# Twenty convolution taps behind the attention, and the layer norm's sums behind later output blocks

## The chip, the cores and the metric

The kernel runs on one core of one Trainium2 chip. The metric is the device time of one execution in microseconds (us), as a median over runs. The engines are called PE (matrix multiplication), DVE (vector), ACT (scalar activation), POOL (GpSimd) and SP (which issues DMA loads).

## The reference

Two layers work on 512 tokens of width 1024. Each layer is a half-step SwiGLU network, a mixer, a second half-step SwiGLU network and a norm. The mixer, which is what the change touches, runs three groups of heads side by side and projects them together:

```python
n = rms_norm(h, mix_norm[l])
p = n @ w_in[l]
u_conv, q, k, v, q_mem = jnp.split(p, splits, axis=-1)
y_conv = conv_module(u_conv, ...)   # GLU, causal depthwise conv of 31 taps over 384 channels, layer norm, silu
y_swa = sliding_window_attention(q, k, v, swa_sinks[l])   # 6 query heads, 2 kv heads, window 128
y_mem = memory_attention(qm, mk, mv)                      # 4 heads over 256 memory tokens
y = jnp.concatenate([y_conv, y_swa, y_mem], axis=-1)
h = h + y @ w_out[l]                                      # 1024 x 1024
```

All is in float32.

## The kernel before

**Layout.** Channels lie on the 128 partitions and the 512 tokens along a row. Matrix products in full precision are made of three products of split operands: `mm3` multiplies hi by hi, lo by hi and hi by lo. A weight is split by ACT (`hi`, a rounded copy) and then by DVE (`lo`, the rest), in `split`; with `split_by_dma` ACT makes both copies and an accumulating DMA from POOL adds the weight to the second.

**The mixer.** `ORDER` lists its steps; the last three are `a` (attention), `t` (taps), `s` (swish). The convolution's 384 channels are three tiles `cv[:, 0..2]` of 128 channels. `tap(c, j)` adds tap j to tile c: one DVE instruction over 512 tokens (L947; the first tap of a tile is L944). There are 3 x 31 = 93 taps. `taps` lists them so that mostly two tiles alternate; the first 13 belong to tile 0 alone and the last 18 to tile 2 alone.

The attention goes over ten groups of head pairs (`GROUPS`). For each group PE makes the scores (L785, L779 adds the mask), DVE takes the row maxima (L789, L804), ACT the exponentials (L816), PE transposes (L826), ACT copies back (L828), PE multiplies by the values (L837) into a bank `po`, DVE scales (L849 to L851), PE transposes the result (L860) and ACT and DVE split it (L146, L147) into the operand `y`.

**What sets the order.** Instructions are placed on each engine's queue by a planner, in the order of the program where several are ready. `tc.issue_after(x)` puts an instruction behind x on x's engine, without waiting for it; `queued()` does so behind PE's last product. So PE's order in this stage is that of the program. Taps from number `EARLY` on are put behind `biased[g]`, the DVE instruction that ends the maxima of group g; `LATER` says how many belong to each group.

**The output projection.** It has eight blocks of 128 output channels, d = 0 to 7. The columns of the weight that meet the convolution (`ours`) come last. The other five 128-row pieces of a block are the window heads (`OWN`, three pieces) and the memory heads (`MEMORY`, two); `out_rows(d, rows)` multiplies them into bank `oo[d]`. `out_weights(d)` loads and splits the weight of block d; the split pieces have four buffers, so that of block d + 4 waits until block d is done.

**The layer norm.** `swish` sums the three tiles on POOL (L969, L970), PE multiplies the sum by ones (L974), DVE subtracts the mean (L977), ACT squares, PE sums the squares over channels (L203), POOL takes the power (L194), PE spreads the result to all partitions (L216), ACT copies it (L222), DVE multiplies (L991), ACT applies silu (L992), ACT and DVE split. Output blocks stand between these products in PE's order. Banks: three of `mm`, two of `po`, one `cf`, a ring of two `pt`.

Of the kernel before, what the change touches and what calls it, by code (L numbers as in the profile page):

```python
# [46 lines left out]
ORDER = "c00 c01 c10 c11 q0 q1 q2 q3 Q0 c20 Q1 c21 Q2 v0 v1 Q3 g0 V1 v2 v3 a t s"  # L47

ALONE = 13
EARLY = 62  # L50
LATER = (1, 4, 3, 3, 2, 2, 2, 2, 2)


def cut(v, bits):
# [11 lines left out]
def trunk(ctx: ExitStack, tc: tile.TileContext, xT, memT, pos, w1a, w3a, w2a, w1b, w3b, w2b,  # L66
# [10 lines left out]
    ps_mm = ctx.enter_context(tc.tile_pool(name="ps_mm", bufs=3, space=bass.MemoryType.PSUM))  # L77
    ps_ax = ctx.enter_context(tc.tile_pool(name="ps_ax", bufs=2, space=bass.MemoryType.PSUM))

    turn, tail = [0], [None]  # L80

    def queued():

# [59 lines left out]


    def split(hi, lo, x, on):
        A.activation(hi, x, AF.Copy)  # L146
        on.tensor_tensor(out=lo, in0=x, in1=hi.bitcast(F32), op=ALU.subtract)  # L147

    def split_by_dma(hi, lo, x, src):

# [33 lines left out]
    def blk(k, n=P):  # L184
        return slice(k * n, (k + 1) * n)
# [219 lines left out]
    def ffn(l, w13, w2, x, sums, factors, last, at_product, aside=None, closing=None):  # L405

        def up(f, i):
            ps = bank([P, S], "po" if 2 * f + i in (3, 4) else "mm")  # L410
            project(ps, weights(w13[i][l, f], 1024, V if f == 0 or f < 3 and l == 0 and w13[0] is w1a else G), x)
            return ps

        def gate(pp, R, u, g, hi, lo):
            V.tensor_tensor(out=u, in0=pp[0], in1=R, op=ALU.mult)
            A.activation(u, u, AF.Silu)
            V.tensor_tensor(out=g, in0=pp[1], in1=R, op=ALU.mult)
            V.tensor_tensor(out=g, in0=g, in1=u, op=ALU.mult)
# [12 lines left out]
        while len(products) < at_product:  # L431
            products.append(up(len(products) // 2, len(products) % 2))
        with queued():
            r = sums()
        with queued():
            products.append(up(at_product // 2, at_product % 2))
        with queued():
            gain, R, after = factors(r)
        M = Seven(normed(gain, R))
        with queued():  # L440
            for f in range(0, PLAIN, 2):
                u, v = (tmp.tile([P, 2, S], F32, tag=t, name=t, bufs=n) for t, n in (("u", 1), ("g", 2)))
                for j in range(2):
                    while len(products) < 2 * (f + j) + 2:
                        products.append(up(len(products) // 2, len(products) % 2))
                    gate(products[2 * (f + j) :], R, u[:, j], v[:, j], *g[f + j])
                if not f:
                    M.first()
        M.rest()
        for q, (f0, nf) in enumerate(QUARTERS):  # L450
            ahead = 2 if q + 1 < len(QUARTERS) else 0
            for f in range(f0, f0 + nf + ahead, 2):
                if f not in g:
                    g[f], g[f + 1] = up_pair(l, w13, f, M)
                    if f == PLAIN:
                        with tc.issue_after(M.gated.ins):
                            rescale = after()
            begun = []

            def begin(d):  # L460

                w = weights(w2[l, d, :, f0 * P : (f0 + nf) * P], nf * P, V)
                ps = bank([P, S], "mm")
                for j in range(nf - 2):
                    mm3(ps, at(w, ALL, blk(j)), g[f0 + j], j == 0, False)
                begun.append((ps, w))

            for d in range(KD if ahead or not closing else KD - 2):
                while len(begun) < (d + 1 if ahead or d else 3):
                    with nullcontext() if ahead or d else queued():  # L470
                        begin(len(begun))
                ps, w = begun[d]
                for j in range(nf - 2, nf):
                    mm3(ps, at(w, ALL, blk(j)), g[f0 + j], False, j == nf - 1)
                if not q and rescale:
                    with tc.issue_after((added if d else M.gated).ins):
                        rescale(d)
                added = V.scalar_tensor_tensor(out=h[:, d, :], in0=ps, scalar=0.5, in1=h[:, d, :], op0=ALU.mult, op1=ALU.add)  # L478
                if not ahead:
                    last(d)  # L480
            if closing and not ahead:
                closing(l, f0, nf, g, [at(p, ALL, slice(0, nf * P)) for p in
                                       (weights(w2[l, d, :, f0 * P : (f0 + nf) * P], nf * P, V) for d in range(KD - 2, KD))])
            if aside and not q:
                aside(added)
# [143 lines left out]
    def mixer(l, x, st, last):  # L629
# [12 lines left out]
        scratch = [wst.tile([P, UNIT], F32, tag="aux", name=f"aux{i}", bufs=3) for i in range(3)]  # L642
        uu = tmp.tile([P, 2, S], F32, tag="u", name="uu", bufs=1)
        query = [tmp.tile([P, 2, S], F32, tag="g", name="query", bufs=2) for _ in range(2)]
        rings = {"pr": [uu[:, 0], uu[:, 1], tm("pr", "pr", 1)], "ptb": [scratch[0][:, blk(i, S)] for i in range(2)],
                 "yn": [scratch[1][:, blk(i, CCH)] for i in range(2)], "cv": [scratch[2][:, blk(i, S)] for i in range(2)]}

        def ring(name):
# [11 lines left out]
            return tuple(z.rearrange("p i s -> p (i s)") for z in gated_pair())  # L660


        biased, raised = {}, {}

        def conv_half(c, i):
            nonlocal R
# [88 lines left out]
            with queued():  # L755
                to_columns(qmT[:, :, blk(t)], memory_query(t), 2)

        yy, y = [], []

# [9 lines left out]
        def scored(kind, pairs):  # L769
# [34 lines left out]
                V.tensor_reduce(out=each(nmw, i), in_=pp[i], axis=AX.X, op=ALU.max)  # L804
            V.scalar_tensor_tensor(out=at_(nmw), in0=at_(nmw), scalar=-1.0, in1=rr, op0=ALU.mult, op1=ALU.mult)
            biased[len(biased)] = V.tensor_tensor(out=at_(nmw), in0=at_(nmw), in1=per(nsinks), op=ALU.min)
            G.tensor_tensor(out=at_(esw), in0=at_(nmw), in1=per(sinks), op=ALU.add)
            return pp, W

        def powers(kind, b, c, scores, W):  # L810
# [28 lines left out]
        def scaled(kind, b, po):  # L839

            n = NH if kind == "w" else NM
            rd = sm(n, f"rd{n}", "a", 4)
            if kind == "w":
                e = esw[:, b]
                A.activation(e, e, AF.Exp)
                V.tensor_tensor(out=rd.rearrange("p (c i) -> p i c", i=2), in0=po[:, :, HD].rearrange("p (c i) -> p i c", i=2), in1=e, op=ALU.add)
                V.reciprocal(rd, rd)
            else:
                V.reciprocal(rd, po[:, :, HD])  # L849
            z = ring("yn")[:, 0 : n * HD]  # L850
            V.tensor_tensor(out=heads(z), in0=po[:, :, 0:HD], in1=rd.unsqueeze(2).to_broadcast([P, n, HD]), op=ALU.mult)  # L851
            return z

        def attended(kind, b, z):
# [7 lines left out]
            while c < n:  # L862
                k = CC + c + (0 if kind == "w" else CC)
                m = 2 - k % 2
                hi, lo = at(yy[k // 2], ALL, slice(k % 2, 2), blk(b))
                split(hi, lo, pt[:, c : c + m, :], V)
                c += m

        GROUPS = (("r", (0, 0), (0, 1)), ("r", (1, 0), (1, 1)), ("w", (0, 0), (0, 1), (0, 2)), ("w", (1, 0), (1, 1)), ("w", (2, 0), (2, 1)),
# [7 lines left out]
        def attention():  # L877
# [45 lines left out]
            for r in done:  # L923
                attended(*r)
            out_rows(2, MEMORY)


        OWN, MEMORY = range(CC), range(CC, 5)
        oo, out_w = [], []
# [20 lines left out]
        def taps():  # L950
# [7 lines left out]
            for n, (c, j) in enumerate(turns):  # L958
                n -= EARLY
                group = sum(n >= sum(LATER[:g]) for g in range(1, len(LATER) + 1))  # L960
                with tc.issue_after(biased[group].ins) if n >= 0 else nullcontext():
                    tap(c, j)


# [1 line left out]

        def swish():
            s1 = ring("cv")
            G.tensor_tensor(out=s1, in0=cv[:, 0, :], in1=cv[:, 1, :], op=ALU.add)  # L969
            G.tensor_tensor(out=s1, in0=s1, in1=cv[:, 2, :], op=ALU.add)  # L970
            out_rows(0, OWN)
            pm = bank([P, S], "pt")
            with queued():
                tail[0] = T.matmul(pm, onesq, s1, start=True, stop=True)  # L974
            st = Stat("st")
            for c in range(CC):
                V.scalar_tensor_tensor(out=cv[:, c, :], in0=pm, scalar=-1.0 / CCH, in1=cv[:, c, :], op0=ALU.mult, op1=ALU.add)  # L977
                st.add(cv[:, c, :], last=c == CC - 1)
            out_rows(1, OWN)
            out_rows(2, OWN)  # L980
            out_rows(3, MEMORY)
            with queued():
                r = rms_cols(st, CCH)
            out_rows(3, OWN)
            with queued():
                RL = kept(spread(r), "RL")
            out_weights(4)
            out_rows(4, (*MEMORY, *OWN))
            for c in range(CC):
                s = ring("cv")  # L990
                V.tensor_tensor(out=s, in0=cv[:, c, :], in1=RL, op=ALU.mult)  # L991
                swished.append(A.activation(s, s, AF.Silu, scale=ln_g[:, c : c + 1], bias=ln_b[:, c : c + 1]))  # L992
                split(y[c][0], y[c][1], s, V)
            for d in range(5, KD):
                out_weights(d)
                out_rows(d, (*MEMORY, *OWN))

        for step in ORDER.split():
            f = {"c": conv_half, "q": queries, "Q": query_columns, "v": values, "V": value_columns, "g": begin, "a": attention,
# [8 lines left out]
        for i, own in enumerate(ours):  # L1008
            raw = wst.tile([P, UNIT], F32, tag="raw", name="raw", bufs=3)
            for j in range(2):  # L1010
                nc.sync.dma_start(raw[:, blk(j, CCH)], wout[l, 2 * i + j, :, 0:CCH])
            with tc.issue_after(swished[1].ins if i > 1 else kept.at.ins) if i else nullcontext():
                A.activation(own[0], raw[:, 0 : 2 * CCH], AF.Copy)
                A.activation(own[1], raw[:, 0 : 2 * CCH], AF.Copy, scale=-1.0)
            for j in range(2):
# [183 lines left out]
```

## The time and the profile before

| | |
|---|---|
| median of 3 runs | 1772.33 us (1772.06 to 1772.84) |
| the profiled execution | 1773.87 us, span 1771.7 us |
| granted clock of PE over the span | 0.998 |
| busy share of PE, DVE, ACT, POOL | 99%, 72%, 51%, 11% |
| layer 0's attention, from 446.6 us to 488.6 us | 42.0 us |
| layer 0's output blocks without the convolution's part | 488.6 us to 520.0 us |

An instruction's row in the profile gives its start, its duration, the engine, the line of the kernel, and the tile written and those read; a count (x) merges equal neighbours. Durations of neighbours on an engine overlap a little, so the step from one start to the next is what an instruction costs there. The busy time of PE is modelled from pipelined products.

### The profile page before, as it was taken

To read this page: it belongs to the slowest core of one execution; us is meant where nothing else is said; L and a number is where in the kernel's file an instruction comes from. 1 tells how busy PE (TensorE), PEld (TensorE's weight loads), DVE (VectorE), ACT (ScalarE), POOL (GpSimd) and SP (SyncE) were. 2 spreads that over 40 slices of the span, in tenths; PEclk is the share of its full clock that TensorE was granted. 3 is DMA by queue.
4 is the path that set the end of the run, shared out by engine and by line. 5 is a ranking of instruction groups with operands and counts; after the bars stand their busy time and mean duration, and the time that the engine had idled before them with its cause. 6 is when DMAs were issued, how large, how long until landed. Compare 5 with 4: busy or idle time off the path is not lost.

```text
span 1771.7 us, 28152 instructions
## 1 busy us (share of the span) xinstructions
PE 1750.1 (99%) x11028; PEld 1579.7 (89%) x11028; DVE 1273.9 (72%) x1895; ACT 900.4 (51%) x1371; POOL 196.9 (11%) x220
## 2 busy tenths in 40 slices
PE   8999999999999999999999999999999999999997
PEld 7989999988788989898889898989887889998987
DVE  6969666589947857575678786666898577666755
ACT  6546444365765535353656453545466755353533
POOL 1001000016121000000010010000251210000000
PEclk9999999999999999999999999999999999999999
DMA  9456645266067547465567465642550866574622
GB/s 281 121 162 177 175 133 148 62 191 135 1 177 175 137 138 175 132 170 137 151 141 182 127 179 143 174 124 84 158 127 2 233 136 170 134 179 125 171 75 84
DMA packets 97205, 253.60 MB, mean 143 GB/s; under 512 B 9904, under 2 KB 16304, under 8 KB 97072
## 3 DMA queue, kind: packets, MB, share of 16 engines
q1 hardware_dynamic: 78064, 190.45, 35.4%
q0 software_dynamic: 19008, 61.35, 19.2%
q8 instruction: 87, 1.43, 0.3%
q14 instruction: 46, 0.38, 0.1%
HBM read 249.67 MB, written 2.10 MB: 142 GB/s over the span
## 4 chain that ended last, share of the span: by engine, by line
PE 87%; DVE 9%; ACT 2%; DMA 1%; issue 1%; SPq 0%; DVEq 0%; ACTq 0%
PE mm L177 13%; PE mm L178 12%; PE mm L179 12%; PE po L177 9%; PE po L179 9%; PE po L178 9%; PE pt L177 6%; PE pt L178 6%; PE pt L179 6%; DVE there L947 5%; PE cf L203 1%; PE po L837 1%; DVE nmw L804 1%; DMA raw<-in_wqk 0%; DMA raw<-in_w2b 0%
## 5 line engine op out<-in xcount | busy, mean ns | idle before, releaser
L146 ACT ACTIVATE whi<-raw 128x1024 fp32r<-128x1024 f32 (+3 forms) x346 | 326.3, 946 | 442.5 <-PE mm L178 227.9
L147 DVE TENSOR_TENSOR wlo<-raw,whi 128x1024 fp32r<-128x1024 f32 (+3 forms) x346 | 374.2, 1082 | 137.0 <-ACT whi L146 136.2
L177 PE MATMUL mm<-ghi,whi 128*128 128x512 f32 (+1 forms) x752 | 292.2, 391 | 0.0
L178 PE MATMUL mm<-glo,whi 128*128 128x512 f32 (+1 forms) x752 | 292.1, 388 | 0.0
L179 PE MATMUL mm<-ghi,wlo 128*128 128x512 f32 (+1 forms) x734 | 284.9, 388 | 0.0
L178 PE MATMUL po<-ml,whi 128*128 128x256 f32 x864 | 244.5, 283 | 0.0
L179 PE MATMUL po<-mh,wlo 128*128 128x256 f32 x864 | 244.5, 283 | 0.0
L177 PE MATMUL po<-mh,whi 128*128 128x256 f32 x864 | 244.4, 283 | 0.0
L179 PE MATMUL pt<-xhi,wlo 128*128 128x256 f32 x864 | 243.9, 283 | 0.0
L178 PE MATMUL pt<-xlo,whi 128*128 128x256 f32 x864 | 243.9, 283 | 0.0
L177 PE MATMUL pt<-xhi,whi 128*128 128x256 f32 x864 | 243.3, 283 | 0.1
L478 DVE SCALAR_TENSOR_TENSOR h<-mm,h 128x512 f32<-128x512 f32 x126 | 86.3, 688 | 129.2 <-PE mm L179 129.1
L177 PEld LDWEIGHTS mm<-ghi,whi 128*128 128x128 f32 x752 | 141.4, 188 | 29.2 <-DVE h L478 1.2
L178 PEld LDWEIGHTS pt<-xlo,whi 128*128 128x128 f32 x864 | 165.7, 192 | 0.8
L177 PEld LDWEIGHTS po<-mh,whi 128*128 128x128 f32 x864 | 165.8, 192 | 0.7
L178 PEld LDWEIGHTS po<-ml,whi 128*128 128x128 f32 x864 | 165.8, 192 | 0.6
L178 PEld LDWEIGHTS mm<-glo,whi 128*128 128x128 f32 x752 | 141.4, 188 | 28.0 <-issue 0.5
L177 PEld LDWEIGHTS pt<-xhi,whi 128*128 128x128 f32 x864 | 165.2, 192 | 1.2 <-DVE g L369 0.3
L179 PEld LDWEIGHTS po<-mh,wlo 128*128 128x128 f32 x864 | 165.8, 192 | 0.0
L179 PEld LDWEIGHTS pt<-xhi,wlo 128*128 128x128 f32 x864 | 165.6, 192 | 0.0
L179 PEld LDWEIGHTS mm<-ghi,wlo 128*128 128x128 f32 x734 | 137.9, 188 | 28.4
L947 DVE SCALAR_TENSOR_TENSOR there<-ypad,par,there 128x512 f32<-128x512 f32 x180 | 136.2, 779 | 1.0
(324 smaller groups left out, 3321.5 us busy)
## 6 DMA issues: line engine op xcount, KB each, us to landing
raw<-in_w2a SPq DMA_DIRECT2D x48, 384.0 KB, 3.5
raw<-in_w2b SPq DMA_DIRECT2D x48, 384.0 KB, 3.5
raw<-in_w1b SPq DMA_DIRECT2D x26, 512.0 KB, 3.7
raw<-in_w3b SPq DMA_DIRECT2D x26, 512.0 KB, 4.0
raw<-in_w1a SPq DMA_DIRECT2D x25, 512.0 KB, 3.7
raw<-in_w3a SPq DMA_DIRECT2D x25, 512.0 KB, 3.8
wsum<-in_w1a SPq DMA_DIRECT2D x18, 512.0 KB, 4.5
wsum<-in_w3a SPq DMA_DIRECT2D x18, 512.0 KB, 4.4
```

The lines of the kernel that those rows point to most:

```text
L146: A.activation(hi, x, AF.Copy)
L147: on.tensor_tensor(out=lo, in0=x, in1=hi.bitcast(F32), op=ALU.subtract)
L177: T.matmul(ps, a[0], b[0], start=first, stop=False, **more)
L178: T.matmul(ps, a[0], b[1], start=False, stop=False, **more)
L179: tail[0] = T.matmul(ps, a[1], b[0], start=False, stop=last, **more)
L203: tail[0] = T.matmul(ss[:, t : t + 1], x[:, blk(t)], onec, start=i == t == 0, stop=i == len(st.sums) - 1, skip_group_check=True)
L478: added = V.scalar_tensor_tensor(out=h[:, d, :], in0=ps, scalar=0.5, in1=h[:, d, :], op0=ALU.mult, op1=ALU.add)
L804: V.tensor_reduce(out=each(nmw, i), in_=pp[i], axis=AX.X, op=ALU.max)
L837: tail[0] = T.matmul(po[:, 2 * c + i, :], ptb[:, i, j, :], v, start=(j == 0), stop=(j == nk - 1))
L947: V.scalar_tensor_tensor(out=cv[:, c, :], in0=ypad[:, c, j : j + S], scalar=conv_w[:, c, j : j + 1], in1=cv[:, c, :], op0=ALU.mult, op1=AL ...
```

## The change

- `EARLY` goes from 62 to 59 and `LATER` from 21 taps in all to 14. The next two taps are put behind the attention's last scaling (`ended[-1]`, L851) and the last 18 behind the last split of its results (`turning[-1][1]`, L147).
- The attention's step now ends with the window heads' pieces of blocks 0 to 2, blocks 3 and 4 whole, and the weights of blocks 4 to 7. They stood in `swish`, between the layer norm's products.
- In `swish`, block 5 stands between the mean's product and the column sums, the memory pieces of block 6 between the sums and the spread, the rest of block 6 and block 7 behind it. The column sums use the ring `pt` and not `cf`. A small silu behind the last square brings ACT's table. POOL's first sum goes behind the last group's `esw`. Tile 2's result uses a third buffer.
- The first two pairs of `ours` are copied by ACT behind the attention's last split, the other two behind `swished[2]`, which is now the last split of the result and not the second silu.
- `hold` puts the first weights' split of the next SwiGLU network behind the last subtraction of the mean on DVE, and the second weights' copies behind `swished[2]` on ACT.

```diff
-EARLY = 62
-LATER = (1, 4, 3, 3, 2, 2, 2, 2, 2)
+EARLY = 59
+LATER = (1, 3, 2, 2, 1, 2, 1, 1, 1)
...
         def up(f, i):
             ps = bank([P, S], "po" if 2 * f + i in (3, 4) else "mm")
-            project(ps, weights(w13[i][l, f], 1024, V if f == 0 or f < 3 and l == 0 and w13[0] is w1a else G), x)
+            with tc.issue_after(hold[f].ins) if f in hold else nullcontext():
+                w = weights(w13[i][l, f], 1024, V if f == 0 or f < 3 and l == 0 and w13[0] is w1a else G)
+            project(ps, w, x)
...
             out_rows(2, MEMORY)
-
+            for d in range(4):
+                out_rows(d, (*MEMORY, *OWN) if d > 2 else OWN)
+                out_weights(d + 4)
+            out_rows(4, (*MEMORY, *OWN))
...
-                with tc.issue_after(biased[group].ins) if n >= 0 else nullcontext():
+                behind = biased[group] if group < len(LATER) else ended[-1] if n < sum(LATER) + 2 else turning[-1][1]
+                with tc.issue_after(behind.ins) if n >= 0 else nullcontext():
                     tap(c, j)
...
             s1 = ring("cv")
-            G.tensor_tensor(out=s1, in0=cv[:, 0, :], in1=cv[:, 1, :], op=ALU.add)
+            with tc.issue_after(sunk[-1].ins):
+                G.tensor_tensor(out=s1, in0=cv[:, 0, :], in1=cv[:, 1, :], op=ALU.add)
             G.tensor_tensor(out=s1, in0=s1, in1=cv[:, 2, :], op=ALU.add)
-            out_rows(0, OWN)
             pm = bank([P, S], "pt")
             with queued():
                 tail[0] = T.matmul(pm, onesq, s1, start=True, stop=True)
             st = Stat("st")
             for c in range(CC):
-                V.scalar_tensor_tensor(out=cv[:, c, :], in0=pm, ...)
+                hold[0] = V.scalar_tensor_tensor(out=cv[:, c, :], in0=pm, ...)
                 st.add(cv[:, c, :], last=c == CC - 1)
-            out_rows(1, OWN)
-            out_rows(2, OWN)
-            out_rows(3, MEMORY)
+            out_rows(5, (*MEMORY, *OWN))
             with queued():
-                r = rms_cols(st, CCH)
-            out_rows(3, OWN)
+                r = rms_cols(st, CCH, "pt")
+            with tc.issue_after(st.at.ins):
+                A.activation(sm(1, "silu"), onec, AF.Silu)
+            out_rows(6, MEMORY)
             with queued():
                 RL = kept(spread(r), "RL")
-            out_weights(4)
-            out_rows(4, (*MEMORY, *OWN))
+            out_rows(6, OWN)
             for c in range(CC):
-                s = ring("cv")
+                s = third if c == 2 else ring("cv")
                 V.tensor_tensor(out=s, in0=cv[:, c, :], in1=RL, op=ALU.mult)
-                swished.append(A.activation(s, s, AF.Silu, scale=ln_g[:, c : c + 1], bias=ln_b[:, c : c + 1]))
-                split(y[c][0], y[c][1], s, V)
-            for d in range(5, KD):
-                out_weights(d)
-                out_rows(d, (*MEMORY, *OWN))
+                A.activation(s, s, AF.Silu, scale=ln_g[:, c : c + 1], bias=ln_b[:, c : c + 1])
+                swished.append(split(y[c][0], y[c][1], s, V)[0])
+            hold[1] = swished[2]
+            out_rows(7, (*MEMORY, *OWN))
...
-            with tc.issue_after(swished[1].ins if i > 1 else kept.at.ins) if i else nullcontext():
+            with tc.issue_after(swished[2].ins if i > 1 else turning[-1][0].ins):
                 A.activation(own[0], raw[:, 0 : 2 * CCH], AF.Copy)
```

More of the change, by code (lines that the diff above doesn't have):

```diff
@@ L78, in trunk @@
     ps_ax = ctx.enter_context(tc.tile_pool(name="ps_ax", bufs=2, space=bass.MemoryType.PSUM))
-    turn, tail = [0], [None]
+    turn, tail, hold = [0], [None], {}
     def queued():
@@ L145, in split @@
     def split(hi, lo, x, on):
-        A.activation(hi, x, AF.Copy)
-        on.tensor_tensor(out=lo, in0=x, in1=hi.bitcast(F32), op=ALU.subtract)
+        a = A.activation(hi, x, AF.Copy)
+        return a, on.tensor_tensor(out=lo, in0=x, in1=hi.bitcast(F32), op=ALU.subtract)
     def split_by_dma(hi, lo, x, src):
@@ L449, in ffn @@
         M.rest()
+        hold.clear()
         for q, (f0, nf) in enumerate(QUARTERS):
@@ L644, in mixer @@
         query = [tmp.tile([P, 2, S], F32, tag="g", name="query", bufs=2) for _ in range(2)]
-        rings = {"pr": [uu[:, 0], uu[:, 1], tm("pr", "pr", 1)], "ptb": [scratch[0][:, blk(i, S)] for i in range(2)],
+        third = tm("pr", "pr", 1)
+        rings = {"pr": [uu[:, 0], uu[:, 1], third], "ptb": [scratch[0][:, blk(i, S)] for i in range(2)],
                  "yn": [scratch[1][:, blk(i, CCH)] for i in range(2)], "cv": [scratch[2][:, blk(i, S)] for i in range(2)]}
@@ L660, in spare @@
             return tuple(z.rearrange("p i s -> p (i s)") for z in gated_pair())
-        biased, raised = {}, {}
+        biased, raised, ended, turning = {}, {}, [], []
         def conv_half(c, i):
@@ L756, in value_columns @@
                 to_columns(qmT[:, :, blk(t)], memory_query(t), 2)
-        yy, y = [], []
+        yy, y, sunk = [], [], []
         nmw, esw = (const.tile([P, NT, 2, CC], F32, tag=t, name=t) for t in ("nmw", "esw"))
@@ L806, in scored @@
             biased[len(biased)] = V.tensor_tensor(out=at_(nmw), in0=at_(nmw), in1=per(nsinks), op=ALU.min)
-            G.tensor_tensor(out=at_(esw), in0=at_(nmw), in1=per(sinks), op=ALU.add)
+            sunk.append(G.tensor_tensor(out=at_(esw), in0=at_(nmw), in1=per(sinks), op=ALU.add))
             return pp, W
@@ L850, in scaled @@
             z = ring("yn")[:, 0 : n * HD]
-            V.tensor_tensor(out=heads(z), in0=po[:, :, 0:HD], in1=rd.unsqueeze(2).to_broadcast([P, n, HD]), op=ALU.mult)
+            ended.append(V.tensor_tensor(out=heads(z), in0=po[:, :, 0:HD], in1=rd.unsqueeze(2).to_broadcast([P, n, HD]), op=ALU.mult))
             return z
@@ L865, in attended @@
                 hi, lo = at(yy[k // 2], ALL, slice(k % 2, 2), blk(b))
-                split(hi, lo, pt[:, c : c + m, :], V)
+                turning.append(split(hi, lo, pt[:, c : c + m, :], V))
                 c += m
@@ L976, in swish @@
             for c in range(CC):
-                V.scalar_tensor_tensor(out=cv[:, c, :], in0=pm, scalar=-1.0 / CCH, in1=cv[:, c, :], op0=ALU.mult, op1=ALU.add)
+                hold[0] = V.scalar_tensor_tensor(out=cv[:, c, :], in0=pm, scalar=-1.0 / CCH, in1=cv[:, c, :], op0=ALU.mult, op1=ALU.add)
                 st.add(cv[:, c, :], last=c == CC - 1)
-            out_rows(1, OWN)
-            out_rows(2, OWN)
-            out_rows(3, MEMORY)
+            out_rows(5, (*MEMORY, *OWN))
             with queued():
-                r = rms_cols(st, CCH)
-            out_rows(3, OWN)
+                r = rms_cols(st, CCH, "pt")
+            with tc.issue_after(st.at.ins):
+                A.activation(sm(1, "silu"), onec, AF.Silu)
+            out_rows(6, MEMORY)
             with queued():
                 RL = kept(spread(r), "RL")
-            out_weights(4)
-            out_rows(4, (*MEMORY, *OWN))
+            out_rows(6, OWN)
             for c in range(CC):
-                s = ring("cv")
+                s = third if c == 2 else ring("cv")
                 V.tensor_tensor(out=s, in0=cv[:, c, :], in1=RL, op=ALU.mult)
-                swished.append(A.activation(s, s, AF.Silu, scale=ln_g[:, c : c + 1], bias=ln_b[:, c : c + 1]))
-                split(y[c][0], y[c][1], s, V)
-            for d in range(5, KD):
-                out_weights(d)
-                out_rows(d, (*MEMORY, *OWN))
+                A.activation(s, s, AF.Silu, scale=ln_g[:, c : c + 1], bias=ln_b[:, c : c + 1])
+                swished.append(split(y[c][0], y[c][1], s, V)[0])
+            hold[1] = swished[2]
+            out_rows(7, (*MEMORY, *OWN))
         for step in ORDER.split():
```

## The prediction

> **What bounds the kernel now.** I read the page first (part 1 for the engines, part 4 for the chain), then tables of time windows around one mixer, then the waits of PE there, and last the instructions of each engine in order of time.
>
> ```profile
> PE 1750.1 (99%) x11028; PEld 1579.7 (89%) x11028; DVE 1273.9 (72%) x1895; ACT 900.4 (51%) x1371; POOL 196.9 (11%) x220
> ```
>
> PE is busy for 1750.1 of 1771.7 us, so an edit that leaves PE's instructions as they are can gain only what PE now waits, and loses whatever new wait it gives PE. The table of windows (columns: window, its length, then busy us and instructions of PE, PEld, DVE, ACT, POOL; granted clock; DMA) shows where the waits lie. The first row is layer 0's attention, the second its output blocks up to the convolution's own part, the third 72 products (x73 with one cut at the edge) of that part; the last two are layer 1's attention and output blocks.
>
> ```profile
> 446.60:488.60 42.00, 39.35 (x321) 33.09 (x319) 38.46 (x88) 30.80 (x74) 7.55 (x9) 1.00 0.01 1
> 488.60:520.00 31.40, 31.40 (x151) 25.86 (x151) 13.97 (x23) 17.57 (x26) 9.37 (x10) 1.00 0.57 140
> 520.00:536.30 16.30, 16.30 (x73) 13.49 (x73) 11.59 (x18) 12.11 (x18) 2.59 (x3) 1.00 1.06 291
> 1321.30:1363.50 42.20, 39.46 (x321) 33.13 (x319) 38.64 (x90) 30.96 (x75) 7.57 (x9) 1.00 0.01 1
> 1363.50:1394.90 31.40, 31.40 (x151) 25.83 (x151) 14.74 (x24) 19.07 (x27) 9.37 (x10) 1.00 0.56 140
> ```
>
> The layers are alike, so I work out one and double it. PE waits 42.00 - 39.35 = 2.65 us in the attention and not at all in the output blocks. The waits of PE in the attention's window:
>
> ```profile
> PE pt L826 <- ACT aux L828: 1.3, 2, 0.7
> PE pt L860 <- ACT aux L828: 0.7, 1, 0.7
> PE pt L826 <- DVE glo L147: 0.3, 1, 0.3
> ```
>
> DVE stands behind the first and third: its taps (L947) sit in front of the maxima that ACT needs. Where the taps are now (busy us of that line alone):
>
> ```profile
> 386.00:442.40 56.40, 42.25 (x56) 1.00 0.72 162
> 442.40:481.70 39.30, 18.43 (x25) 1.00 0.01 1
> 481.70:491.10 9.40, 7.45 (x10) 1.00 0.01 2
> ```
>
> With the three first taps (L944) some 59 lie ahead of the first group's maxima, 24 (25 with one cut) within the groups, 10 after the last group's.
>
> **The change, part by part.** *Taps.* 59 stay ahead, 14 lie within, 20 follow: ten leave the attention. Of the 20, two come behind the last scaling (L851) and 18 behind the last split of the attention (L147). Those 18 are the lone channel's, each adding to the result of the one before. The price of such a tap differs from that of alternating channels; DVE in order of time, with POOL's first sum (L969) as the fourth row:
>
> ```profile
> 386.15 2.33 DVE L947 SCALAR_TENSOR_TENSOR there<-ypad,par,there 128x512 f32<-128x512 f32 x3
> 429.48 4.72 DVE L947 SCALAR_TENSOR_TENSOR there<-ypad,par,there 128x512 f32<-128x512 f32 x7
> 461.73 1.64 DVE L947 SCALAR_TENSOR_TENSOR there<-ypad,par,there 128x512 f32<-128x512 f32 x1
> 461.56 1.26 POOL L969 TENSOR_TENSOR aux<-there 128x512 f32<-128x512 f32 x1
> ```
>
> Three dependent taps take 2.33, so with 0.75 for the last the step is (2.33 - 0.75) / 2 = 0.79; seven alternating ones give (4.72 - 0.74) / 6 = 0.66. I use 0.79.
>
> *The attention.* What it can give is between 0 and 2.65 us a layer. The 0.7 before L860 is the last group's copy out of the bank and has no tap in front, so I take the rest, 2.65 - 0.75 = 1.9.
>
> *PE's cover behind it.* The change puts output blocks 0 to 4 ahead of the mean's product (L974). PE before, in order of time:
>
> ```profile
> 486.60 0.44 PE L860 MATMUL pt<-cst,aux 128*128 128x128 f32 x2 [0.75 <-ACT aux L828]
> 488.58 0.48 PE L177 MATMUL mm<-ghi,whi 128*128 128x512 f32 x1
> 491.46 0.55 PE L860 MATMUL pt<-cst,aux 128*128 128x128 f32 x3
> 495.27 1.02 PE L974 MATMUL pt<-aux,onesq 128*128 128x512 f32 x2
> 501.62 0.95 PE L203 MATMUL cf<-onesq,st 128*128 128x1 f32 x8
> 505.50 1.05 PE L216 MATMUL pt<-cst,rsq 128*128 128x128 f32 x8
> ```
>
> Let T be the first output product, now 488.58. One 128-row piece is three products, 3 x 16.30 / 72 = 0.68 us. Ahead of L974 stand 2 + 2 + 2 pieces of the memory heads, 3 + 3 + 3 of the window heads and two whole blocks of 5: 25 pieces, 17.0 us, and 0.3 for the transposes. PE reaches L974 at T + 17.3. The queued order holds it there: everything behind, block 5 first, waits with it.
>
> *DVE's way to the same point.* DVE, POOL and ACT before:
>
> ```profile
> 490.19 0.75 DVE L947 SCALAR_TENSOR_TENSOR there<-ypad,par,there 128x512 f32<-128x512 f32 x1
> 493.10 0.42 DVE L147 TENSOR_TENSOR glo<-pt,ghi 128x256 fp32r<-128x256 f32 x1 [0.45 <-ACT ghi L146]
> 496.01 0.82 DVE L147 TENSOR_TENSOR wlo<-raw,whi 128x640 fp32r<-128x640 f32 x1 [2.48 <-ACT whi L146]
> 496.75 1.88 DVE L977 SCALAR_TENSOR_TENSOR there<-pt,there 128x512 f32<-128x512 f32 x3
> 491.08 1.28 POOL L970 TENSOR_TENSOR aux<-aux,there 128x512 f32<-128x512 f32 x1 [8.53 <-DVE there L947]
> 503.74 1.02 POOL L194 TENSOR_TENSOR rsq<-ms,nhalf 128x4 f32<-128x4 f32 x1 [11.37 <-DVE ms L209]
> 497.47 0.63 ACT L236 ACTIVATE st<-there 128x512 f32<-128x512 f32 x1 [1.49 <-DVE there L977]
> ```
>
> The last transposes come behind four memory pieces, at T + 2.7; from them to the end of the last split is 493.10 + 0.42 - 491.46 = 2.1, so the 18 taps start at T + 4.8. They take 17 x 0.79 + 0.75 = 14.2: T + 19.0. Among them come the splits of output weights 4 to 7, now written ahead of the taps, each as soon as a finished block frees its buffer: blocks 0, 1, 2 and 3 end at about T + 6.5, 8.5, 10.5 and 14, all before the taps do. A split holds DVE for 0.74 (496.01 to 496.75), of which 0.13 fills the gap of a dependent pair: 4 x 0.6 = 2.4, T + 21.4. Then POOL's second sum: 0.15 from the tap's end (490.94) to 491.08, 1.28, and 0.1 to PE: L974 can start at T + 22.9. PE waits 22.9 - 17.3 = 5.6 us. Low end: only split 4, which block 4 itself needs, falls among the taps: 3.8. High end: each split costs its full 0.82 (+0.9), and POOL's first sum, now behind the last group's, holds up a split as it held the tap of 1.64 against 0.75 (+0.9): 7.4. I take 5.6: dependent taps and four ready splits are what the code says, and the first sum falls into the 0.45 and longer gaps of DVE there. [...]
>
> *The clock.* No wait like this is in the trace except the start:
>
> ```profile
> 6.07 0.80 PE L177 MATMUL mm<-xhi,whi 128*128 128x512 f32 x1 [6.07 <-ACT xhi L156]
> 10.44 0.63 PE L179 MATMUL mm<-xhi,wlo 128*128 128x512 f32 x1
> 10.86 0.63 PE L178 MATMUL mm<-xlo,whi 128*128 128x512 f32 x1
> 12.36 0.39 PE L178 MATMUL mm<-xlo,whi 128*128 128x512 f32 x1
> 1763.00:1764.00 1.00, 0.18 (x2) 0.57 0.64 207
> ```
>
> After 6.07 us without work, products stepped by 0.42 (10.44 to 10.86) instead of 16.30 / 72 = 0.23 until 12.36: 6.3 us at half speed, 2.9 lost. The last row, at the kernel's end, shows the granted clock fall to 0.57 once PE thins out. Bounds: 0 (waits of 0.75 us leave the clock at 1.00) and 2.9. Between them by length of wait: (5.6 - 0.75) / (6.07 - 0.75) x 2.9 = 2.6 a layer, which I take. [...]
>
> *Behind L974.* Block 5 covers 5 x 0.68 = 3.4 and L974 itself 1.1 (495.27 to 496.3); what it covers is L977 (1.88), the last square (0.63) and one addition, at most 1.1 + 1.88 + 0.63 + 0.7 = 4.3 < 4.5: nothing. Between the column sums and the spread the way is 505.50 - 501.62 = 3.9 at most, of which POOL's power is 1.02; block 6's two memory pieces and the sums themselves (1.8) cover 3.2, and PE now fills the rest with pieces that it would do anyway: 0 to 0.7, taken as 0, since the row's 3.9 ends with PE's work, not with POOL's (503.74 + 1.02 = 504.76). The rest of block 6 and block 7 cover 8 x 0.68 = 5.4 us of the way from the spread to the first result, whose pieces are
>
> ```profile
> L991 DVE TENSOR_TENSOR aux<-there,RL x6: 683/692/694, 507.2 to 1389.1; 128x512 f32<-128x512 f32 x6
> L992 ACT ACTIVATE aux<-aux,par 128x512 f32<-128x512 f32 x6 | 4.6, 805 | 0.0
> L146 ACT ACTIVATE ghi<-aux 128x512 fp32r<-128x512 f32 x6 | 3.7, 615 | 0.0
> L147 DVE TENSOR_TENSOR glo<-aux,ghi 128x512 fp32r<-128x512 f32 x6 | 4.1, 689 | 11.1 <-ACT ghi L146 11.1
> 508.68 1.28 ACT L992 ACT_TABLE_LOAD   x1
> ```
>
> 0.69 + 0.81 + 0.62 + 0.69 = 2.8 and the copy of the spread: nothing. The table load (1.28) leaves that way for the time of the column sums; PE did not wait for it, so no gain. Sums and spread move from one bank to the ring of two; each next user starts after its release by that order. SP issues weights 4 to 7 earlier and POOL's accumulating DMAs for the own weights come before its second sum or after, with ACT's copies behind the attention; they have over 15 us until block 0's last pieces: nothing. The next FFN's weights are held behind L977 and the last result; their PE slot lies 16.30 us later: nothing.
>
> **The sum.** 5.6 - 1.9 + 2.6 = 6.3 us a layer, 12.6 in all. The profiled execution took 1773.87 (span 1771.7), so 1786.5 by its clock; it stands 1.5 above the median of the runs, and against that 1772.33 + 12.6 = 1784.9.
>
> **The rivals.**
> *The clock holds.* Then 2 x 3.7 = 7.4: 1779.7. For it: no row shows what a wait between 0.75 and 6.07 us does. Against it: the end of the trace, where the clock fell with short products still running.
> *The two cancel.* The wait is at its low end, 3.8, all 2.65 come back and the clock holds: 2 x 1.15 = 2.3: 1774.6, no measurable change. Against it: it needs three of the splits to come late.
> *Faster: the attention is DVE's.* DVE is busy 38.46 of 42.00 there. If it set the pace, ten taps at 0.75 and POOL's 0.9 would shorten the attention by 8.4, more than the wait of 5.6: 2 x -2.8 gives 1766.7. It decides from 5.6 us on. Against it: PE is busy for 39.35 and cannot shrink by more than it waits.
> *Longer.* A split written between two taps is not ready, because ACT or a DMA is behind, and the taps queue behind it on DVE: at the upper ends, 7.4 - 0 + 2.9 = 10.3 a layer, 1792.9.
>
> **How the numbers follow.** Forecast 0.52, clock holds 0.22, cancel 0.09, faster 0.10, longer 0.07. A measurement of this kernel can tell about 0.2% (3.5 us) from no change: slower 0.52 + 0.22 + 0.07 = 0.81, same 0.09, faster 0.10. The range leaves out cancel and faster (0.19) and reaches into the longer case: 1775 to 1790; the forecast's own is 1781 to 1789.
>
> **What the changed profile would show.** Right: in both layers an idle PE ahead of L974 of 4 to 7 us, released by POOL's L970, with L947 and four L147 of 640 columns alternating on DVE before it; the attention's window near 40 us; a granted clock below 1.00 just behind the wait; no PE wait at L203, L216 or the own pieces. Wrong: L970 done before PE gets there (the taps or splits cost less), or an attention shorter than 39 us.

## The result, and the profile after

The changed kernel takes 1791.34 us (median of 4 runs, 1788.76 to 1792.3), the kernel before beside it 1772.59 (1772.06 to 1773.94): ratio 1.0102, 95% interval 1.0085 to 1.012. It is slower, as predicted, but by 18.75 us instead of 12.6, and 1.3 us above the range. The profiled execution took 1792.3, its span is 1789.7. In the changed code the taps are L954, POOL's sums L978 and L979, the mean's product L982, its subtractions L985, ACT's copies of the own weights L1019 and L1020, POOL's DMAs for them L1022. The own weights, here as in the prediction, are the convolution's columns of the output weights (`ours`, four pairs, each for two blocks), not the window heads' `OWN`.

Below is the table of windows (columns as in the prediction), cut at the same events in each kernel. First the kernel before: for each layer the attention, then everything from the first output product to the next SwiGLU network's column sums.

```profile
446.39:488.58 42.19, 39.54 (x321) 33.24 (x321) 38.67 (x89) 31.00 (x75) 7.55 (x9) 1.00 0.01 1
488.58:541.80 53.22, 53.22 (x247) 43.91 (x247) 30.36 (x48) 32.56 (x48) 12.83 (x14) 1.00 0.74 194
1321.11:1363.46 42.35, 39.61 (x322) 33.24 (x321) 38.82 (x89) 31.15 (x75) 7.57 (x9) 1.00 0.01 1
1363.46:1416.71 53.25, 53.25 (x248) 43.90 (x248) 30.36 (x48) 32.68 (x48) 12.82 (x14) 1.00 0.72 194
```

Then the changed kernel, five rows a layer: attention; first output product to the mean's product L982; from there to the column sums L203; to the spread L216; to the next network's column sums.

```profile
447.17:487.05 39.88, 38.92 (x321) 33.25 (x321) 27.97 (x72) 30.64 (x73) 5.42 (x8) 1.00 0.01 1
487.05:511.31 24.26, 17.66 (x80) 14.26 (x79) 19.16 (x29) 6.68 (x10) 6.56 (x6) 0.92 0.47 123
511.31:517.19 5.88, 5.88 (x17) 3.92 (x18) 3.62 (x5) 2.89 (x4) 0.00 (x0) 0.75 0.24 42
517.19:520.48 3.29, 3.29 (x24) 2.81 (x23) 0.16 (x1) 0.63 (x1) 1.03 (x1) 1.00 0.46 164
520.48:552.50 32.02, 30.18 (x129) 24.51 (x129) 19.68 (x30) 22.60 (x35) 7.17 (x8) 0.95 0.81 211
...
1331.83:1371.72 39.89, 38.92 (x322) 33.26 (x321) 27.68 (x72) 30.63 (x73) 5.44 (x8) 1.00 0.01 1
1371.72:1395.96 24.24, 17.66 (x81) 14.27 (x80) 19.16 (x29) 6.68 (x10) 6.56 (x6) 0.91 0.49 125
1395.96:1403.11 7.15, 7.15 (x18) 5.02 (x19) 3.62 (x5) 2.79 (x4) 0.00 (x0) 0.59 0.28 52
1403.11:1406.32 3.21, 3.21 (x24) 2.73 (x22) 0.57 (x2) 1.48 (x2) 1.03 (x1) 1.00 0.29 114
1406.32:1436.39 30.07, 28.78 (x130) 23.37 (x129) 19.28 (x30) 21.89 (x34) 7.16 (x8) 1.00 0.83 216
```

The attention gave back 2.3 and 2.5 us. The second row of layer 0 is 24.26 long with 17.66 of work: PE stands still 6.6 us ahead of L982. The row behind it has a clock of 0.75 in layer 0 and 0.59 in layer 1. The last row of each layer has 1.84 and 1.29 us in which PE is idle. PE's waits of the whole execution name both places:

```profile
PE pt L982 <- POOL aux L979: 13.2, 2, 6.6
PE pt L179 <- DMA whi<-in_wout: 3.1, 2, 1.8
```

How the wait at L982 came about, in order of time, from the attention's last split on (T, the first output product, is now 487.05): DVE, POOL, PE, and then three rows of ACT.

```profile
491.48 0.43 DVE L147 TENSOR_TENSOR glo<-pt,ghi 128x256 fp32r<-128x256 f32 x1 [0.45 <-ACT ghi L146]
491.82 2.32 DVE L954 SCALAR_TENSOR_TENSOR there<-ypad,par,there 128x512 f32<-128x512 f32 x3
494.41 0.82 DVE L147 TENSOR_TENSOR wlo<-raw,whi 128x640 fp32r<-128x640 f32 x1 [0.27 <-ACT whi L146]
...
502.85 0.83 DVE L147 TENSOR_TENSOR wlo<-raw,whi 128x640 fp32r<-128x640 f32 x1 [1.00 <-ACT whi L146]
503.59 6.26 DVE L954 SCALAR_TENSOR_TENSOR there<-ypad,par,there 128x512 f32<-128x512 f32 x8
510.00 1.26 POOL L979 TENSOR_TENSOR aux<-aux,there 128x512 f32<-128x512 f32 x1 [3.50 <-DVE there L954]
511.31 2.08 PE L982 MATMUL pt<-aux,onesq 128*128 128x512 f32 x2 [6.60 <-POOL aux L979]
...
500.61 0.85 ACT L1019 ACTIVATE whi<-raw 128x768 fp32r<-128x768 f32 x1 [2.14 <-DMA raw<-in_wout]
501.36 0.83 ACT L1020 ACTIVATE whi<-raw 128x768 fp32r<-128x768 f32 x1
502.10 0.72 ACT L146 ACTIVATE whi<-raw 128x640 fp32r<-128x640 f32 x1
```

The taps start at T + 4.8, the four splits stand among them, eight dependent taps take 6.26. The fourth split waits 1.00 on DVE, with eight taps behind it: its first half stands on ACT behind the own weights' copies, which waited 2.14 for their load.

The second wait is in the own weights. ACT copies the last two pairs behind the last result, POOL issues their DMAs, and PE, which needs for block 6 what the last of them brings, stands still:

```profile
528.83 0.83 ACT L1019 ACTIVATE whi<-raw 128x768 fp32r<-128x768 f32 x1
532.32 2.13 POOL L1022 DMA_DIRECT2D whi<-in_wout  x2
543.70 0.50 PE L179 MATMUL pt<-ghi,whi 128*128 128x512 f32 x1 [1.84 <-DMA whi<-in_wout]
545.01:548.43 3.42, 3.42 (x10) 2.57 (x9) 2.11 (x4) 1.51 (x3) 0.00 (x0) 0.50 1.06 245
```

From the issue to PE's start are 11.4 us, and the last row, of the table of windows, shows half the clock for 3.42 us behind a wait of 1.84.

### The profile page after: what moved, and what is told of

Same layout as the page of the kernel before. It is cut to its first block, busy times and chain, and to the rows that moved or that the text cites. A ratio compares the mean times of both kernels' runs of the same rounds, so it can differ in the third digit from the quotient of the medians.

```text
span 1789.7 us, 28146 instructions
## 1 busy us (share of the span) xinstructions
PE 1756.4 (98%) x11028; PEld 1582.7 (88%) x11028; DVE 1276.5 (71%) x1895; ACT 901.8 (50%) x1373; POOL 196.4 (11%) x220
## 4 chain that ended last, share of the span: by engine, by line
PE 90%; DVE 4%; DMA 3%; ACT 2%; issue 1%; POOL 0%; SPq 0%; DVEq 0%; POOLq 0%; ACTq 0%
PE mm L177 13%; PE mm L178 13%; PE mm L179 13%; PE po L179 8%; PE po L177 8%; PE po L178 8%; PE pt L179 6%; PE pt L178 6%; PE pt L177 6%; PE po L841 1%; DMA whi<-in_wout 1%; PE mm L789 1%; PE pt L830 1%; PE cf L177 1%; PE cf L179 1%
## 5 line engine op out<-in xcount | busy, mean ns | idle before, releaser
L147 DVE TENSOR_TENSOR wlo<-raw,whi 128x1024 fp32r<-128x1024 f32 (+3 forms) x346 | 374.3, 1083 | 127.4 <-ACT whi L146 123.2
L954 DVE SCALAR_TENSOR_TENSOR there<-ypad,par,there 128x512 f32<-128x512 f32 x180 | 134.7, 770 | 1.6
```

Of the source, the lines that this page charges most:

```text
L147: return a, on.tensor_tensor(out=lo, in0=x, in1=hi.bitcast(F32), op=ALU.subtract)
L954: V.scalar_tensor_tensor(out=cv[:, c, :], in0=ypad[:, c, j : j + S], scalar=conv_w[:, c, j : j + 1], in1=cv[:, c, :], op0=ALU.mult, op1=AL ...
```

## The experiments

Each ratio is against the kernel before on the same chip (medians 1774.3 us for the first four kernels below; 1773.54 for the two with ScalarE held, the one with the own weights early as well, and the first version with a middle number of taps; 1773.57 for the other three). Theory A at first was that the taps behind the attention, with the half clock behind their wait, are the whole cost but for the late own weights.

**The taps where they were.** All else as changed.

```diff
-EARLY = 59
-LATER = (1, 3, 2, 2, 1, 2, 1, 1, 1)
+EARLY = 62
+LATER = (1, 4, 3, 3, 2, 2, 2, 2, 2)
...
+behind = biased[group]
```

> The changed kernel with the taps where they were before: 62 ahead, 21 within the groups, 10 behind the last group's maxima; all else of the change stays (order of output blocks, ring of banks, own weights, holds). Theory A (the loss is DVE's 18 taps and four splits behind the attention, which keep the mean's product L974, now L982, waiting, plus a half clock after that wait, plus late own weights): PE does not wait at L982, no half clock there, the attention is 42 us again, and only the wait for the own weights (1.3 to 1.8 us a layer) is left: 1776, between 1773 and 1779. Theory B (the moved order of the layer norm's products and the shared ring of banks cost time themselves): waits at the column sums, the spread or the banks stay, and the time stays above 1783.

Measured: 1792.82 us, ratio 1.0104 (1.0089 to 1.012). The wait at L982 is gone and the time is the same. PE's waits, and ACT in order of time:

```profile
PE pt L203 <- ACT sq L236: 12.3, 2, 6.2
...
508.10 0.63 ACT L236 ACTIVATE sq<-there 128x512 f32<-128x512 f32 x1
515.59 1.06 ACT L146 ACTIVATE whi<-raw 128x1024 fp32r<-128x1024 f32 x1 [6.86 <-DMA raw<-in_w1b]
516.55 0.61 ACT L236 ACTIVATE sq<-there 128x512 f32<-128x512 f32 x1
...
512.80:523.00 10.20, 5.79 (x21) 5.21 (x22) 1.71 (x3) 4.12 (x5) 1.03 (x1) 0.50 0.34 86
```

The last of the three squares stands on ACT behind the copy of the next network's first weight, which waits 6.86 us for its load; the column sums need the square. The clock falls here too, to 0.50 for 10.20 us, as the last row (of the table of windows, layer 0) shows. In the changed kernel the same copy stands ahead of the squares, and is over just before they could begin:

```profile
512.28 1.06 ACT L146 ACTIVATE whi<-raw 128x1024 fp32r<-128x1024 f32 x1 [7.81 <-DMA raw<-in_w1b]
514.15 0.63 ACT L236 ACTIVATE st<-there 128x512 f32<-128x512 f32 x1 [0.82 <-DVE there L985]
```

So a second bound of nearly the same length lies beneath the first, and taking away the taps alone changes nothing in the time. A in this form fell. The time is where theory B put it, but B's reason, a cost of the new order itself, is refuted further down by a run that has this order and no loss.

**The own weights early.** ACT's copies of the last two pairs behind the last square, their DMAs behind the power on POOL; taps as changed.

```diff
-with tc.issue_after(swished[2].ins if i > 1 else turning[-1][0].ins):
+with tc.issue_after(squared[0].ins if i > 1 else turning[-1][0].ins):
...
+with tc.issue_after(rsq.at.ins) if i > 1 else nullcontext():
```

> The changed kernel, with ACT's copies of the last two pairs of own weights behind the last square instead of behind the last result's split, and POOL's accumulating transfers of these behind its power. Theory A: these transfers are issued some 9 us earlier, PE's wait for them (1.8 and 1.3 us) and the second half-clock stretch of layer 0 (3.4 us long, 1.7 lost) go; the wait at L982 stays at 6.6: 1786.5, between 1785 and 1788.5. Rival C (the transfers are late because the queues are full, not because they are issued late): the wait moves with them and the time stays at 1790 to 1792.

Measured: 1788.65 us, ratio 1.0082 (1.0065 to 1.0098). No wait for the own weights is left. Windows from L982 to L203, and the last stage, of layer 0:

```profile
510.12:517.45 7.33, 7.33 (x18) 5.11 (x19) 3.62 (x5) 5.56 (x8) 0.00 (x0) 0.58 0.37 83
...
520.65:548.87 28.22, 28.22 (x130) 23.54 (x130) 18.84 (x30) 18.82 (x30) 7.93 (x9) 1.00 0.91 216
```

The last stage falls from 32.02 to 28.22 (layer 1: 30.07 to 28.24), so the late DMAs cost 3.8 and 1.8 us. That they were issued late, and not that the queues were full (rival C), is shown by the wait's being gone. Layer 0 lost part of it again in a longer stretch at half clock behind L982 (7.33 for 5.88). The time is 0.15 above theory A's range, and its interval overlaps that of the changed kernel: the evidence is the trace, not the total.

**PE kept at work ahead of the mean's product.** 24 products of 512 columns whose result nothing uses.

```diff
+idle = bank([P, S], "cf")
+with queued():
+    for _ in range(24):
+        tail[0] = T.matmul(idle, out_w[4][0][:, blk(0)], y[CC][0], start=True, stop=True)
 pm = bank([P, S], "pt")
```

> The changed kernel, with 24 unused products of 512 columns (24 x 0.23 = 5.4 us) put on PE just ahead of L982, into a bank that is overwritten later, so that PE works while DVE finishes the taps. Theory A (the wait of 6.6 us halves the clock after it: 1.5 us lost in layer 0 and 2.9 in layer 1 of the changed kernel's profile): L982 starts at the same time, the clock stays at 1.00 behind it, and 3 to 5 us go: 1787, between 1785.5 and 1788.5. Rival D (the half clock behind the wait is hidden by the layer norm's own way, which is long): no change, 1790 to 1792.

Measured: 1791.59 us, ratio 1.0099 (1.0084 to 1.0114). L982 to L203 in both layers:

```profile
510.31:515.15 4.84, 4.55 (x17) 3.12 (x17) 3.62 (x5) 2.62 (x4) 0.00 (x0) 1.00 0.32 57
...
1396.30:1402.33 6.03, 6.03 (x18) 4.20 (x19) 3.62 (x5) 2.88 (x4) 0.00 (x0) 0.72 0.22 38
```

In layer 0 the clock holds (1.00) and the stage is 1.04 us shorter than without the fill. In layer 1 the fourth split came later (the mean's product 25.78 us behind the first output product, not 24.24), a wait of 2.7 us stayed, and the clock fell all the same (0.72). The total is the "no change" of rival D, but layer 0 speaks against D's reason: the half clock is not hidden there. What the two shorter stages gave, 1.0 and 1.1 us, went to the later split (1.5) and to a last stage that was 0.6 us longer in layer 1. So the half clock costs at least 1 us where it was taken away, but filling did not pay.

**The taps' new place alone, in the kernel before.** Nothing else of the change.

> The kernel before with the new places of the taps alone (59, 14, 2 behind the last scaling, 18 behind the last split); output blocks, banks and own weights as before. Theory A: PE reaches the mean's product L974 6.7 us after its first output product, and DVE's taps let it start at about 21: PE waits some 14 us a layer, less 2.4 that the attention gives, plus 2 to 3 for the clock: 14 a layer, 1800.6, between 1795 and 1806. If the attention is what DVE sets, and the taps were the good part of the change (rival E), the time is below 1785.

Measured: 1803.66 us, ratio 1.0166 (1.0151 to 1.0181).

```profile
PE pt L975 <- POOL aux L971: 29.1, 2, 14.6
```

With the old order of blocks (L975 is there the mean's product) the wait is 14.6 us a layer, 8.0 more than in the change. There PE has 10.9 us more to do ahead of this product (17.66 against 6.78), and the splits among the taps put it off by 2.9 (24.26 against 21.33).

**ScalarE held, with the new taps and with the old.** The next network's first copies behind the last result on ACT.

```diff
-with tc.issue_after(hold[f].ins) if f in hold else nullcontext():
+with (tc.issue_after(hold[f].ins) if f in hold else nullcontext(),
+      tc.issue_after(hold[1].ins) if f == 0 and hold else nullcontext()):
```

> Change made, and ScalarE's copies of the next FFN's first two weights are queued behind the last copy of the convolution's result, so they can no longer stand ahead of the squares. Theory A (two bounds, one beneath the other: first the taps that follow, then ScalarE's queue behind late weight loads; only the upper one shows): the taps still end last, so the wait ahead of the mean's product stays at 6 to 7 us a layer and the time at about 1790.5 (1788 to 1792.5). Rival B (ScalarE's queue alone is what the change costs): about 1777.

> The same hold on ScalarE, and the taps where they were before the change. Theory A: with both bounds gone PE waits neither at the mean's product nor at the column sums; what is left is the late own weights, about 2.2 us a layer by the run with the taps back alone: 1777 (1774 to 1780). Rival B expects the same as A here and differs in the run before this one. Rival C (the layer norm's steps simply have too little work over them in the new order, whatever the queues hold): a wait of some 5 us a layer stays at the column sums or the spread: over 1783.

Measured: 1799.02 (ratio 1.0139, 1.0122 to 1.0157) and 1784.84 (1.006, 1.0045 to 1.0075). The waits of the first, then of the second:

```profile
PE pt L983 <- POOL aux L980: 13.3, 2, 6.7
PE cf L203 <- DVE st L248: 4.3, 2, 2.2
...
PE cf L203 <- DVE st L248: 4.3, 2, 2.2
PE pt L179 <- DMA whi<-in_wout: 3.7, 2, 2.2
```

Held, with the new taps, PE still waits 6.7 us at the mean's product (here L983): the copies that stood ahead of the squares are not the whole cost. With the old taps that wait and the one of 6.2 us are both gone: theory A in its second form, two bounds one beneath the other, and the time falls by 14.2 from the one run to the other. Both totals are some 8 us above what I expected. Of this 4.3 is a new wait, 2.2 us a layer at the next network's column sums; in the 12 us behind it layer 0's clock was 0.72 and 0.86, which by an estimate (with the clock at 1.00 or at the 0.50 of the rows above, 0.72 is 56% of the time at 0.50, and half of that time is lost) is 3.4 and 1.7 us more. The hold alone does not make this wait: in the next run it stays, and the wait is gone. What makes it is the hold together with the late own weights, whose copies stand on ACT ahead of the held ones. The rest of the 8 us was not followed.

**The own weights early as well.** Held, taps back, and the second experiment's edit.

> As the run before, and the own weights' last two pairs are copied behind the last square and their DMAs issued behind the power on GpSimd. Theory A: nothing of the change's cost is left; new order of blocks with no wait behind the attention: 1773.5 (1771.5 to 1776), the same as before. Rival C: over 1781.

Measured: 1777.2 us, ratio 1.0019 (1.001 to 1.0029), still 1.2 above theory A's range. Between the first output product and the spread PE waits nowhere in either layer; what is left lies in the last stage, 29.67 and 31.00 long. DVE, then ACT:

```profile
525.51 0.69 DVE L1030 TENSOR_TENSOR h<-mm,h 128x512 f32<-128x512 f32 x1 [2.49 <-PE mm L179]
...
526.70 1.06 ACT L151 ACTIVATE whi<-raw 128x1024 fp32r<-128x1024 f32 x1 [3.22 <-PE mm L179]
527.66 1.04 ACT L152 ACTIVATE wlo<-raw 128x1024 fp32r<-128x1024 f32 x1
528.61 0.71 ACT L156 ACTIVATE xhi<-h,gn 128x512 fp32r<-128x512 f32 x1
```

Block 0 is ready at 526.2, and its operand (L156) starts on ACT at 528.61, behind the copies of a weight. ACT had stood waiting 3.22 us to begin these; the row names a product of PE as what ended that wait, where the next expectation speaks of a late load. The two were not told apart.

**That copy too behind its turn.** As above, and the second unit's second weight behind the fourth block's operand.

```diff
+      tc.issue_after(hold["x"].ins) if f == i == 1 and hold else nullcontext()):
```

> As the run with the taps back, ScalarE held and the own weights early; besides, ScalarE's copies of the next FFN's second unit's second weight stand behind the fourth block's operand and not ahead of the first. Theory D (what the run before lost, 1.5 and 2.8 us in the last stage, is ScalarE standing in that copy for a late load while the first operands of the next FFN are ready behind it): last stage 28.2 to 28.6 us, PE no longer waits for the operands' splits, 1773.5 (1772 to 1775.5), no different from before. Rival E (the waits come from the splits of the FFN's first weights on VectorE): unchanged at 1777.

Measured: 1773.63 us, ratio 0.9999 (0.999 to 1.0008). So it was the copy's place on ACT. Attention and the rest, layer by layer:

```profile
445.37:487.46 42.09, 39.30 (x321) 33.33 (x321) 38.81 (x89) 30.99 (x75) 7.53 (x9) 1.00 0.01 1
487.46:540.80 53.34, 53.34 (x247) 43.85 (x247) 30.30 (x48) 32.47 (x49) 13.90 (x15) 1.00 0.74 192
1320.20:1362.97 42.77, 39.38 (x322) 33.33 (x321) 39.48 (x91) 31.48 (x75) 7.54 (x9) 1.00 0.00 1
1362.97:1416.33 53.36, 53.36 (x248) 43.85 (x248) 30.30 (x48) 32.60 (x49) 13.41 (x15) 1.00 0.72 186
```

This has the change's new order of blocks and its banks, and takes the time of before: the order itself costs next to nothing (53.34 against 53.22), and gives nothing.

**A middle number of taps.** Looking for a version that beats both: the holds of the run with the own weights early as well (without the last one, of the copy just above), 59 taps ahead, 20 within the attention, 14 behind; weights 6 and 7 split behind the last tap.

```diff
+LATER = (1, 3, 2, 2, 2, 2, 2, 3, 3)
...
+with tc.issue_after(lasttap[0].ins):
+    for d in range(6, KD):
+        out_weights(d)
```

> All holds of the run before (the own weights' second pair too), with 59 taps ahead, 20 within the attention and 14 behind it, and the splits of output weights 6 and 7 behind the last tap instead of between taps. Worked out: the last split T + 4.8, 12 dependent taps of 0.79 and two splits of 0.6 make T + 15.5, GpSimd's sum T + 17.0, PE gets there at T + 17.3: no wait. Of the attention's 2.3 us some part comes back. Theory A: 1771 (1768.5 to 1774.5), a little faster than before. Rival (any tap within the attention costs it its full gain): 1773.5. Rival C: over 1781.

Measured: 1781.93 us, ratio 1.0044 (1.0032 to 1.0056); in its trace PE waited 1.08 for POOL's sum, which had two DMA issues ahead of it and then ran beside DVE's splits (1.93 us, in place of 1.26). It also waited 3.2 us in all for the operands' splits, as in the run whose copy had not yet been moved. The profiled execution took 1778.31, and the runs spread from 1777.14 to 1787.85; what the slower of them lost was not followed. A second version put those DMAs behind the sum and added the hold of that copy, so its gain cannot be put down to either alone; a third also moved six taps behind the last maxima:

> 59 taps ahead, 20 within and 14 behind, splits of output weights 6 and 7 behind the last tap, all holds, and the own weights' first DMAs on GpSimd behind its second sum. Theory D: the wait of 1.1 us at the mean's product in the earlier version of this run came from those two DMA issues ahead of the sum; it goes; stages 41.2 + 17.6 + 4.4 + 3.2 + 28.4 = 94.8 against 95.5 before: 1772.2 (1770 to 1775). Rival (the sum is slowed by the splits on VectorE as before): a wait of 0.7 us stays, 1773.6.

> As the run before, but of the 20 taps within the attention 14 stand where the change put them and six stand behind the last group's maxima, where VectorE has gaps of 0.5 to 1.5 us. Theory F (only taps ahead of maxima cost the attention anything): attention 40.4, sum 94.0, 1770.6 (1768.5 to 1774), faster than both. Rival G (taps ahead of the last splits and scalings cost as much as those ahead of maxima): attention 41.2 or more, 1772 to 1775.

Measured: 1773.79 (1.0001, 0.9992 to 1.0009) and 1776.44 (1.0013, 1.0004 to 1.0022). In the second version the wait at the mean's product is gone (0.04 us are left) and the attention is 41.17 in both layers, 1.0 and 1.2 shorter than before. What follows it takes that back: 54.52 us in layer 0 (53.22 before), most of it in a last stage of 29.20 (28.25 in the run that takes the time of before), and 53.73 in layer 1 (53.25 before). In the third version the attention took 41.02 and 42.78. In layer 0 the taps behind the last maxima cost it as much as those ahead of them (G). In layer 1 the clock fell as well, to 0.50 from 1361.67 to 1368.50, which makes the attention and the stage behind it 1.8 and 1.1 us longer than in layer 0 and puts this execution's time, 1776.53, above both theories' ranges. Below, layer 0 of the second version, then layer 1 of the third:

```profile
447.10:488.27 41.17, 39.28 (x322) 33.37 (x321) 31.09 (x78) 30.69 (x73) 6.64 (x9) 1.00 0.00 1
488.27:542.79 54.52, 53.81 (x247) 43.77 (x247) 39.42 (x59) 32.45 (x49) 14.34 (x15) 1.00 0.71 184
...
1360.98 0.44 PE L866 MATMUL pt<-cst,aux 128*128 128x128 f32 x2 [0.81 <-ACT aux L834]
1361.67:1368.50 6.83, 6.80 (x27) 5.92 (x27) 3.65 (x9) 1.15 (x3) 0.00 (x0) 0.50 0.00 0
```

No version was measurably faster than the kernel before.

## Why the prediction was right in its sign and short in its size

Layer by layer, in us, from the stages above. What the stages behind the attention take in the new order without these waits is read from layer 0 of the run that takes the time of before: 17.58, 4.30, 3.21 and 28.25. The sums are of unrounded terms.

| term | predicted | layer 0 | layer 1 |
|---|---|---|---|
| attention | -1.9 | -2.3 | -2.5 |
| wait at the mean's product | 5.6 | 6.7 | 6.7 |
| half clock behind it | 2.6 | 1.6 | 2.9 |
| late own weights, with their half clock | 0 | 3.8 | 1.8 |
| order of blocks | 0 | 0.2 | 0.1 |
| sum | 6.3 | 9.9 | 9.0 |

The layers sum to 18.9; the spans differ by 18.0, and the 0.9 between lies outside the two mixers and was not followed.

*The wait.* Right in mechanism, 1.1 too small. The two runs with ScalarE held price it with its clock and the attention's gain: 14.2 us for both layers, where the table has 13.1. PE got to L982 at T + 17.7 (predicted 17.3). Taps started at T + 4.8 as predicted; the last ended at 503.59 + 6.26 = 509.85, T + 22.8, where I had T + 21.4. Of the 1.4, 1.00 is the fourth split, which was not ready. The other 0.4 is in part the first split's wait of 0.27. That is the "longer" rival in part: I had bounded the splits by DVE's own price of a split and had not asked what stands ahead of their first half on ACT. That this rival's time, 1792.9, lies nearest to the measured one is luck: its mechanism gave some 1.3 of the 9 to 10 us a layer.

*The own weights: the step that failed.* This is the largest term that is missing from the sum: 3.8 and 1.8 us, put at nothing. I wrote that they "have over 15 us until block 0's last pieces". That holds for the first two pairs. The change ties the other two to the last result, and those I had not costed: they were copied from 527.4, and POOL issued the last DMAs at 532.32, behind one of the next network's (L349). The trace after gives the own DMAs between 527 and 546 a median of 9.8 us from issue to landing; the kernel before issued its last two pairs at 513.26 and 515.25, 16 to 17 us earlier than the changed one did (529.23 and 532.32). The early copies removed the wait, which shows the cause. Of the signs that I had named for a right prediction, "no PE wait at" the own pieces is the one that did not come.

*The next network's weights: a step that was wrong and cost nothing here.* That the first weights are "held behind L977" is true on DVE only. ACT's half of the first split was free to go ahead of the squares, and did. In the changed kernel the taps hide it; with the taps out of the way it made PE wait 6.2 us a layer, which the prediction had at nothing.

*The clock.* Chosen 2.6, measured 1.6 and 2.9, within my bounds; that it fell in both layers speaks for the forecast and against the rival in which it holds. My scale by the length of the wait is wrong, though (below): the waits were equally long in both layers (6.60 and 6.58 us), and that 2.6 lies between the two losses is luck.

*The attention.* 2.3 and 2.5 for 1.9: the wait of 0.75 at L860, which I left standing, fell to 0.5. The second rival, that the two cancel, fails with this term and the wait: the attention gave nearly all it could, but the wait was not at its low end. The rival in which the attention is DVE's bound is refuted: DVE's busy time there fell by 10.7 us (38.67 to 27.97) and the time by 2.3.

## What to carry to other kernels

Beneath a wait that an edit takes away or covers another of nearly the same length can lie (here 6.6 and 6.2 us). Before calling an edit's cover sufficient, look at what else stands in the queue of every engine that the chain passes, the copies that wait for a load above all. A hold binds one engine; a split over two engines, or three with its DMA, needs one on each. And when undoing one suspected part changes nothing, undo a second with it before dropping the first; and when an edit adds a hold, look for what the held work then delays.

## What the runs showed of the hardware

The granted clock fell to 0.50 around waits far shorter than the 6.07 us of the start. In the changed kernel it was at 0.50 for 6.82 us (507.47 to 514.29) in layer 0, of which PE worked 2.98, and for 10.24 us (1391.52 to 1401.76) in layer 1, of which it worked 5.80. Both stretches begin within PE's wait ahead of L982 (504.71 to 511.31 and 1389.38 to 1395.96), not behind it. Behind the wait of 1.84 us it was at 0.50 for 3.42, and in the last run behind one of 0.81 us, in the midst of short products, for 6.83. Waits of 0.75 in the kernel before left it at 1.00 (446.39 to 488.58), and so did the wait of 1.29 us in layer 1's last stage of the changed kernel (1406.32 to 1436.39). With the 10.20 us of the run with the taps back, the five lengths lie within 1% of one, two or three times 3.42. In these runs, then, the length of the wait alone sets neither whether the clock falls (1.29 us left it, 0.81 did not) nor for how long (6.82 and 10.24 us, with waits of 6.60 and 6.58); what does was not found.

```profile
507.47:514.29 6.82, 2.98 (x5) 1.75 (x6) 3.14 (x6) 1.20 (x2) 1.26 (x1) 0.50 0.79 190
1391.52:1401.76 10.24, 5.80 (x12) 3.94 (x13) 6.49 (x9) 2.79 (x4) 1.26 (x1) 0.50 0.56 130
```
